# A second-layer head pair in another TensorE order: gate halves between key, value and query products, attention steps at written places

## The chip, the cores and the metric

One core of one Trainium2 chip. The metric is device time in microseconds (us): the median of 3 runs of the kernel before is 784.22 us (781.72 to 784.26). Engines are named as in the profile: PE is TensorE, DVE is VectorE, ACT is ScalarE, POOL is GpSimd, SP is the engine that issues the weight loads.

## The reference, cut to what matters

The model is a two-layer trunk over 512 tokens of width 1024. The first layer is an mLSTM mixer with memory cross-attention. From its output a compressed latent for keys and values is computed, and the second layer is latent attention with 8 heads:

```python
h = rmsnorm(x, norm_g)
q_lat, z, mq, mz = split_cols(h @ w_in, [Q_LORA, B_WIDTH, MEM_WIDTH, MEM_WIDTH])
q = (rmsnorm(q_lat, q_lat_g) @ w_q_up).reshape(bsz, s, B_HEADS, QK_HEAD)
q = rmsnorm(q, q_gain)                      # then rope on the last 64 columns
attn = chunk_causal_attention(q, k_sh, v_sh).reshape(bsz, s, B_WIDTH)
y_b = attn * jax.nn.silu(z)
return x + jnp.concatenate([y_b, y_mem], axis=-1) @ w_out
```

Keys and values (k_sh, v_sh) come from `rmsnorm(c_kv) @ w_kv_b`. A head has 128 plain columns and 64 rope columns in q and k, and 128 in v. The mask is causal in chunks of 64, worked in query blocks of 128. Only the order of this second layer's work is changed, no arithmetic.

## The kernel before, in words

All products run in fp32r with operands split in a high and a low part: `prod` issues high by high, high by low and low by high, three matmuls for each block of the sum. A weight is loaded by SP into `wr` (2 buffers), multiplied by a gain on POOL where there is one (L146), and split by ACT (high part, `wh`, L130) and DVE (low part, `wl`, L131), 2 buffers each.

The second layer works on 4 pairs of heads. What a pair needs is written as Python generators; each `yield` ends a step:

- `b_kv(p)`: keys and values of a pair, 4 steps, one for each 128 tokens (acc tiles of 512 columns). ACT and DVE take them out, norm them, and POOL scales the rope part (L911).
- `b_q(p)`: queries, 4 steps (384 columns). DVE copies the plain part (L949), ACT copies the rope part and sums squares (L951, L190), POOL applies rope (L845 to L848).
- `b_z(p, c)`: the gate product of head c, in two halves of 4 blocks each, then silu (L203, L204).
- `b_T(p, name, h)`: PE transposes of keys or queries (L923) into a `tp` tile, then ACT and DVE split them into `qk` tiles. With h = 2 it is the rope part of both heads (L928); its way out is longer: ACT copy (L931), for keys a DVE copy (L933), and a DVE subtraction (L934), once for each head.
- `b_attn(p)`: attention in 9 steps. Step n computes the scores of unit n (softmax on DVE, ACT, DVE: L977, L322, L324, L332, L333, L335), transposes the probabilities of unit n - 2 into a `tp` tile (L987; taken out by L991 or L993) and, when a head's three units are through, multiplies by the values (L1000).

PSUM tiles are few: `acc` has 4 buffers, `att` 2, `tp` 2. The transposed probabilities of a head lie in one tile of tag `e`, which has one buffer, so head 1's first block can be taken out only when head 0's product with the values is done. These lines hold the spacing of the attention steps:

```python
units = [(h, tiles) for h in range(2) for tiles in ((0, 1), (2,), (3,))]
lag = 2
for n in range(len(units) + lag + 1):
    if n < len(units):
        scores(*units[n])
    if 0 <= n - lag < len(units):
        trans(*units[n - lag])
    m = n - lag - 1
    if m >= 0 and m % 3 == 2:
        values(m // 3)
    yield
```

`weave(main, side, plan)` runs one step of main, then plan[i] steps of side. Tile's scheduler orders each engine's instructions from its own timeline, except inside `tc.manual_schedule(engines={PE})`, where PE keeps the order of the program. In the kernel before, pair 0, pair 1 and the attention of pair 0 are ordered by the scheduler; the products of pairs 2 and 3, the attention of pairs 1 to 3 and the output projection are in the written order.

Of the kernel before, what the change touches and what calls it, by code (L numbers as in the profile page):

```python
# [40 lines left out]
def weave(main, side, plan=()):  # L41
    for i, _ in enumerate(main):
        for _ in range(plan[i] if i < len(plan) else 1):
            next(side, None)
    for _ in side:
        pass


def chain(*gens):
    for g in gens:  # L50
        yield from g
# [8 lines left out]
def trunk(ctx: ExitStack, tc: tile.TileContext, pv_d, pos_d, x_d, memT_d, wmem_d, wg_d, wa_d, woa_d,  # L60
# [131 lines left out]
    def proj_T(w, hT, ps):  # L192
        for k in range(0, KT, 4):
            prod([(ps, sub(hT, slice(None), j), sub(w, slice(None), j), False) for j in range(k, k + 4)],
                 k == 0, k == 4)
            yield
# [568 lines left out]
    mT, _ = load_memT(False)  # L765
# [113 lines left out]
    def b_z(p, c):  # L879
        d = pairs.setdefault(p, {})  # L880
        if c == 0:
            d["z"] = st([P, 2, S], ("z4", "mv")[p % 2])
        sz = d["z"]
        w = load(wb_d[8 + 2 * p + c], KT, P, pv[:, _PV["bn"]:_PV["bn"] + KT])
        ps = acc()
        yield from proj_T(w, hT, ps)
        silu2(sz[:, c], ps)
        yield

    def b_kv(p):  # L890
        d = pairs.setdefault(p, {})
        kns = st([P, NT, 256], "s4", 2)
        krs = s2([P, NT, P])
        d["v"] = vt = st([P, NT, 256], ("gt", "mkT")[p % 2])
        d["ks"] = kns, krs
        w = load(wkvb_d[p], 2, 512)
        for t in range(NT):
            ps = acc()
            prod([(ps, lat(ckT, k, t), sub(w, slice(None), k), True) for k in range(2)], True, True)
            V.tensor_copy(kns[:, t], ps[:, 0:256])  # L900
            A.activation(vt[:, t], ps[:, 256:512], AF.Copy)
            ss = tiny([P, 2])
            for h in range(2):
                sqsum(kns[:, t, h * P:(h + 1) * P], ss[:, h:h + 1])
            V.tensor_scalar(ss, ss, sspe[:, t:t + 1], None, op0=ALU.add)
            r2 = tiny([P, 2])
            rpow(r2, ss, 1.0 / 192, EPS, 2)
            for h in range(2):
                hs = slice(h * P, (h + 1) * P)
                V.tensor_scalar(kns[:, t, hs], kns[:, t, hs], r2[:, h:h + 1], None, op0=ALU.mult)  # L910
                G.tensor_scalar(krs[:, t, h * 64:(h + 1) * 64], kb[:, t], r2[:, h:h + 1], None, op0=ALU.mult)  # L911
            yield

    def b_T(p, name, h):

        d = pairs[p]
        main, rp = d["ks" if name == "k" else "qs"]
        tp = tps()
        if h < 2:
            pair = d.setdefault(name + "n", [])  # L920
            pair.append(st([P, 2, S], "qk", 4, F32R))
            for t in range(NT):
                PE.transpose(tp[:, t * P:(t + 1) * P], main[:, t, h * P:(h + 1) * P], ident)  # L923
            split(pair[h][:, 0], pair[h][:, 1], tp, gg[:, 2:3] if name == "k" else None)
            return
        d[name + "r"] = r = st([P, 2, S], "v", 2, F32R)
        for t in range(NT):
            PE.transpose(tp[:, t * P:(t + 1) * P], rp[:, t], ident)  # L928
        for h in range(2):
            hs, other = slice(h * 64, (h + 1) * 64), slice(64 - h * 64, 128 - h * 64)  # L930
            A.activation(r[hs, h], tp[hs], AF.Copy)  # L931
            if name == "k":
                V.tensor_copy(r[other, h], r[hs, h])  # L933
            V.tensor_tensor(out=(kl[hs, h] if name == "k" else r[other, h]), in0=tp[hs], in1=r[hs, h].bitcast(F32),  # L934
                            op=ALU.subtract)

    def b_q(p):
        d = pairs[p]
        d["rq"] = rqp = st([P, NT, 2], "rqp", 2)
        w = load(wqup_d[p][:, 0:768], 2, 384), load(wqup_d[p][:, 768:1152], 1, 384)  # L940
        qns = st([P, NT, 256], "s4", 2)
        qrs = s2([P, NT, P])
        d["qs"] = qns, qrs
        ssq = tiny([P, NT, 2])
        for t in range(NT):
            ps = acc([P, 384])
            prod([(ps, lat(qlT, k, t), sub(w[k // 2], slice(None), k % 2), True) for k in range(3)], True, True)
            p3 = ps.rearrange("p (a b) -> p a b", a=2)
            V.tensor_copy(qns[:, t].rearrange("p (a b) -> p a b", a=2), p3[:, :, 0:P])  # L949
            qx = st([P, 2, 64], "qx", 2)  # L950
            A.activation(qx, p3[:, :, P:192], AF.Copy)  # L951
            for h in range(2):
                sqsum(p3[:, h], ssq[:, t, h:h + 1])
            rope(qrs[:, t].rearrange("p (a b) -> p a b", a=2), qx, 0, st([P, 2, 64], "qt", 2),
                 lambda i, a, b, t=t: tabs[:, i, t, a:b].unsqueeze(1).broadcast_to([P, 2, b - a]))
            yield
        rpow(rqp.rearrange("p a b -> p (a b)"), ssq.rearrange("p a b -> p (a b)"), 1.0, 192 * EPS, 8)

    def b_attn(p):
        kn, qn, kh, qr, vt, sz, rqp = (pairs[p][n] for n in ("kn", "qn", "kr", "qr", "v", "z", "rq"))  # L960
        prs, pTs = {}, {}

        def scores(h, tiles):
            ps = acc() if p < 3 and tiles[0] == 2 else att()
            views = []
            for j, i in enumerate(tiles):
                n = (i + 1) * P
                m = max(n, 256)
                qs = slice(i * P, (i + 1) * P)
                pt = ps[:, j * 256:j * 256 + m]  # L970
                prod([(pt, (qn[h][:, 0, qs], qn[h][:, 1, qs]), (kn[h][:, 0, :m], kn[h][:, 1, :m]), True)],
                     True, False)
                PE.matmul(pt, qr[:, h, qs], kh[:, h, :m], start=False, stop=False)
                PE.matmul(pt, qr[:, h, qs], kl[:, h, :m], start=False, stop=True)
                views.append(pt[:, :n])
            for v in views:
                V.memset(v[0:64, -64:], -1.0e30)  # L977
            prs[h, tiles] = softmax_rows(views, rqp[:, tiles[0]:tiles[-1] + 1, h])

        def trans(h, tiles):  # L980
            if tiles[0] == 0:
                pTs[h] = st([P, 1280], "e", 1)
            tp = tps()
            n = 0
            for i, pr in zip(tiles, prs[h, tiles]):
                for c in range(i + 1):
                    PE.transpose(tp[:, n:n + P], pr[:, c * P:(c + 1) * P], ident)  # L987
                    n += P
            o = tiles[0] * (tiles[0] + 1) // 2 * P
            if tiles[0] == 2:  # L990
                A.activation(pTs[h][:, o:o + n], tp[:, :n], AF.Copy)  # L991
            else:
                V.tensor_copy(pTs[h][:, o:o + n], tp[:, :n])  # L993

        def values(h):
            ps = att()
            for i in range(NT):
                for c in range(i + 1):
                    o = (i * (i + 1) // 2 + c) * P
                    PE.matmul(ps[:, i * P:(i + 1) * P], vt[:, c, h * P:(h + 1) * P], pTs[h][:, o:o + P],  # L1000
                              start=c == 0, stop=c == i)
            gate_out(yT, 2 * p + h, ps, sz[:, h])
# [11 lines that stand above are left out]
            yield  # L1014

    def b_pair(p):
        yield from b_kv(p)
        yield from b_q(p)
        todo = [(n, h) for h in range(3) for n in "kq"]
        for _ in chain(b_z(p, 0), b_z(p, 1)):  # L1020
            yield
            b_T(p, *todo.pop(0))

    drain(b_pair(0))
    weave(b_pair(1), b_attn(0), (0,) * 5)
    x1b = []

    def residual():
        x1b.extend(load_x(x1_d, nc.sync))
        yield from ()  # L1030
# [4 lines left out]
        A.dma_start(out_d[t * P:(t + 1) * P, half * 512:(half + 1) * 512], o)  # L1035

    with tc.manual_schedule(engines={mybir.EngineType.PE}):
        weave(chain(*(b_pair(p) for p in range(2, 4)), residual(), out_proj(wob_d, yT, b_done)),
              chain(*(b_attn(p) for p in range(1, 4))), ((0,) * 5 + (1,) * 9) * 2)


_OUTS = [((1, S, D), 'float32')]
# [100 lines left out]
```

## Time and profile before

| | |
|---|---|
| median of 3 runs | 784.22 us (781.72 to 784.26) |
| profiled execution | 780.85 us |
| its span in the trace | 779.1 us |
| PE busy | 760.0 us (98%) |
| DVE busy | 497.6 us (64%) |
| ACT busy | 401.7 us (52%) |
| POOL busy | 185.1 us (24%) |

A profile is one execution. Its span runs from the first to the last recorded instruction; 1.75 us of the execution's time lie around it. PE's busy time is modelled from pipelined matmuls, so the reader should look at its idle stretches and at what ended them more than at the 98%.

### The profile page before, as it was taken

What the parts mean: (1) busy time and instruction counts of PE and PEld (TensorE: products, weight loads), DVE (VectorE), ACT (ScalarE), POOL (GpSimd) and SP (SyncE); (2) the same over time, 40 slices, a digit from 0 to 9 for tenths busy, and PEclk for the clock granted to TensorE, in tenths of its full rate; (3) what the DMA queues carried; (4) which work ended last, traced back from release to release, by engine and by line L of the source; (5) the groups of instructions that cost most, each with busy time, mean ns of one, the idle gap of its engine ahead of it and who ended that gap; (6) DMA issues with size and microseconds to landing.
All of it is one profiled execution on the core that took longest, in us unless ns stands there. A gap on an engine that the chain in (4) does not pass through costs nothing.

```text
span 779.1 us, 11004 instructions
## 1 busy us (share of the span) xinstructions
PE 760.0 (98%) x3956; PEld 651.6 (84%) x3956; DVE 497.6 (64%) x978; ACT 401.7 (52%) x940; POOL 185.1 (24%) x286
## 2 busy tenths in 40 slices
PE   7999999999999999999999999999998999999997
PEld 5798887888888888888888888999787888888886
DVE  7753499738768746756434545497678787885432
ACT  4855656436546435546334636467656565644220
POOL 5311010001110101001002175250975461900000
PEclk9999999999999999999999999999999999999999
DMA  9322220322132223225434532222322111511141
GB/s 336 125 89 82 82 82 29 108 82 82 54 109 67 95 84 107 76 87 161 158 141 150 174 109 84 60 62 59 100 65 58 55 52 36 187 55 55 60 157 54
DMA packets 25190, 75.35 MB, mean 97 GB/s; under 512 B 2864, under 2 KB 3504, under 8 KB 25136
## 3 DMA queue, kind: packets, MB, share of 16 engines
q1 hardware_dynamic: 23568, 72.39, 28.1%
q10 hardware_dynamic: 1440, 2.25, 0.8%
q8 instruction: 31, 0.51, 0.3%
q14 instruction: 23, 0.19, 0.1%
q0 software_dynamic: 128, 0.01, 0.0%
HBM read 70.44 MB, written 4.19 MB: 96 GB/s over the span
## 4 chain that ended last, share of the span: by engine, by line
PE 82%; DVE 11%; ACT 2%; issue 1%; POOL 1%; DVEq 0%; ACTq 0%; POOLq 0%
PE acc L160 45%; PE acc L165 23%; PE att L160 3%; PE att L1000 2%; PE att L165 2%; DVE wl L131 2%; PE tp L987 1%; DVE tiny L322 1%; DVE kl L613 1%; PE tp L923 1%; DVE s L335 1%; PE att L699 1%; PE att L700 1%; PE att L698 1%; DVE s L910 1%
## 5 line engine op out<-in xcount | busy, mean ns | idle before, releaser
L131 DVE TENSOR_TENSOR wl<-wr,wh 128x1024 fp32r<-128x1024 f32 (+5 forms) x117 | 140.5, 1202 | 156.8 <-ACT wh L130 132.6
L130 ACT ACTIVATE wh<-wr 128x1024 fp32r<-128x1024 f32 (+5 forms) x117 | 117.8, 1009 | 138.8 <-PE acc L160 114.4
L160 PE MATMUL acc<-wh,hTl 128*128 128x512 f32 (+4 forms) x352 | 123.6, 361 | 0.0
L160 PE MATMUL acc<-wh,hTh 128*128 128x512 f32 (+4 forms) x352 | 123.2, 362 | 0.3 <-ACT hTh L133 0.3
L160 PE MATMUL acc<-hTh,wh 128*128 128x512 f32 x256 | 101.6, 397 | 0.0
L160 PE MATMUL acc<-hTl,wh 128*128 128x512 f32 x256 | 100.5, 393 | 0.0
L165 PE MATMUL acc<-wl,hTh 128*128 128x512 f32 (+4 forms) x352 | 88.6, 359 | 0.0
L160 PE MATMUL acc<-wh,yTh 128*128 128x512 f32 x192 | 75.0, 394 | 0.0
L160 PE MATMUL acc<-wh,yTl 128*128 128x512 f32 x192 | 74.8, 390 | 0.0
L160 PEld LDWEIGHTS acc<-wh,hTh 128*128 128x128 f32 x352 | 65.2, 188 | 9.8 <-ACT hTh L133 0.7
L160 PEld LDWEIGHTS acc<-wh,hTl 128*128 128x128 f32 x352 | 65.5, 188 | 8.2
L165 PE MATMUL acc<-hTh,wl 128*128 128x512 f32 x256 | 69.3, 391 | 0.0
L165 PEld LDWEIGHTS acc<-wl,hTh 128*128 128x128 f32 x352 | 61.7, 188 | 8.9
L146 POOL TENSOR_TENSOR wr<-wr,pv 128x1024 f32<-128x1024 f32 (+2 forms) x24 | 42.6, 1776 | 87.7 <-DMA wr<-in_wb_dram 44.7
L165 PEld LDWEIGHTS acc<-hTh,wl 128*128 128x128 f32 x256 | 47.8, 188 | 9.9
L160 PEld LDWEIGHTS acc<-hTl,wh 128*128 128x128 f32 x256 | 48.2, 188 | 9.1
L160 PEld LDWEIGHTS acc<-hTh,wh 128*128 128x128 f32 x256 | 48.1, 188 | 9.1
L165 PE MATMUL acc<-wl,yTh 128*128 128x512 f32 x192 | 53.3, 389 | 0.0
L185 POOL TENSOR_SCALAR tiny<-tiny 128x2 f32<-128x2 f32 (+4 forms) x36 | 9.9, 276 | 164.3 <-ACT junk L190 52.3
L160 PE MATMUL acc<-wh,u 128*128 128x384 f32 (+1 forms) x160 | 38.9, 367 | 3.4 <-ACT junk L190 2.3
L165 PEld LDWEIGHTS acc<-wl,yTh 128*128 128x128 f32 x192 | 36.0, 188 | 7.4
L160 PEld LDWEIGHTS acc<-wh,yTh 128*128 128x128 f32 x192 | 36.1, 188 | 7.2
(285 smaller groups left out, 1467.9 us busy)
## 6 DMA issues: line engine op xcount, KB each, us to landing
wr<-in_wa_dram SPq DMA_DIRECT2D x46, 512.0 KB, 3.2
wr<-in_wb_dram SPq DMA_DIRECT2D x16, 512.0 KB, 3.5
wr<-in_woa_dram SPq DMA_DIRECT2D x12, 512.0 KB, 3.3
wr<-in_wob_dram SPq DMA_DIRECT2D x12, 512.0 KB, 3.2
wr<-in_wmem_dram SPq DMA_DIRECT2D x8, 512.0 KB, 3.3
yTh<-in_wmem_dram SPq DMA_DIRECT2D x6, 512.0 KB, 6.9
s<-in_memT_dram SPq DMA_DIRECT2D x8, 256.0 KB, 3.9
yTl<-in_x_dram SPq DMA_DIRECT2D x4, 512.0 KB, 9.2
```

The lines of the kernel that those rows point to most:

```text
L130: A.activation(hi, src, AF.Copy)
L131: V.tensor_tensor(out=lo, in0=src, in1=hi.bitcast(F32), op=ALU.subtract)
L146: G.tensor_tensor(out=r3, in0=r3, in1=gain.unsqueeze(2).broadcast_to([P, nk, ncol]), op=ALU.mult)
L160: PE.matmul(ps, x if lhs else w_[0], w_[0] if lhs else x, start=start and id(ps) not in seen, stop=False)
L165: PE.matmul(ps, a_[0] if lhs else w_[1], w_[1] if lhs else a_[0], start=False, stop=stop and left[id(ps)] == 0)
L185: G.tensor_scalar(t, ss, mul, add, op0=ALU.mult, op1=ALU.add)
L322: V.tensor_reduce(mx[:, j:j + 1], ps, axis=AX.X, op=ALU.max)
L335: V.tensor_scalar(out[j], out[j], sm[:, j:j + 1], None, op0=ALU.mult)
L613: V.scalar_tensor_tensor(out=u[:, d:], in0=raw[:, :S - d], scalar=col("cw", (3 - d) * 16 + j), in1=u[:, d:], op0=ALU.mult, op1=ALU.add)
L698: PE.matmul(ps[:, :258], ph[:, blk(c, i)], v[0][:, c], start=c == 0, stop=False)
L699: PE.matmul(ps[:, :258], low(c, i), v[0][:, c], start=False, stop=False)
L1000: PE.matmul(ps[:, i * P:(i + 1) * P], vt[:, c, h * P:(h + 1) * P], pTs[h][:, o:o + P], start=c == 0, stop=c == i)
```

## The change

In the kernel before, a pair's steps are: 4 of keys and values, 4 of queries, then 6 of gates with one `b_T` after each of them (k0, q0, k1, q1, k2, q2). The attention steps of the pair before follow steps 5 to 13, one each.

After, a pair has 14 steps in a written list: gate half, kv, kv, gate half, kv, kv, q, q, q, q, then k0 and k2, gate half with k1 and q0, gate half with q2, and q1. A gate's second half and its silu are now one step. The attention steps are placed by a plan: two behind step 5, one each behind steps 6, 7 and 8, two behind step 9, none behind 10, one each behind 11 and 12, none behind 13. Pair 1 and the attention of pair 0 move into the part in which PE keeps the written order.

```diff
@@ def b_z(p, c):
-        yield from proj_T(w, hT, ps)
+        m = proj_T(w, hT, ps)
+        next(m)
+        yield
+        drain(m)
         silu2(sz[:, c], ps)
         yield
@@ def b_pair(p):
-        yield from b_kv(p)
-        yield from b_q(p)
-        todo = [(n, h) for h in range(3) for n in "kq"]
-        for _ in chain(b_z(p, 0), b_z(p, 1)):
+        kv, q, z = b_kv(p), b_q(p), chain(b_z(p, 0), b_z(p, 1))
+        for g, *ts in ((z,), (kv,), (kv,), (z,), (kv,), (kv,), (q,), (q,), (q,), (q,), (q, ("k", 0), ("k", 2)),
+                       (z, ("k", 1), ("q", 0)), (z, ("q", 2)), (q, ("q", 1))):
+            next(g, None)
+            for t in ts:
+                b_T(p, *t)
             yield
-            b_T(p, *todo.pop(0))
 
     drain(b_pair(0))
-    weave(b_pair(1), b_attn(0), (0,) * 5)
@@ with tc.manual_schedule(engines={mybir.EngineType.PE}):
-        weave(chain(*(b_pair(p) for p in range(2, 4)), residual(), out_proj(wob_d, yT, b_done)),
-              chain(*(b_attn(p) for p in range(1, 4))), ((0,) * 5 + (1,) * 9) * 2)
+        weave(chain(*(b_pair(p) for p in range(1, 4)), residual(), out_proj(wob_d, yT, b_done)),
+              chain(*(b_attn(p) for p in range(4))), (0, 0, 0, 0, 0, 2, 1, 1, 1, 2, 0, 1, 1, 0) * 3)
```

## Rows read from the trace of the kernel before

**Rows 1.** Busy time of each engine, three stretches; then granted clock, DMA.

```profile
541.90:607.50 65.60, 61.76 (x325) 53.71 (x324) 47.13 (x111) 42.43 (x133) 44.60 (x74) 0.97 0.22 67
607.50:655.30 47.80, 45.63 (x287) 40.50 (x286) 39.59 (x91) 28.72 (x82) 20.35 (x36) 1.00 0.17 52
655.30:696.20 40.90, 39.72 (x235) 34.73 (x234) 32.86 (x82) 25.01 (x75) 21.14 (x36) 1.00 0.35 115
```

**Rows 2.** Waits of PE, 540 to 697 us: total us, times, longest.

```profile
PE acc L160 <- ACT junk L190: 2.3, 1, 2.3
PE tp L987 <- DVE s L335: 1.6, 4, 0.6
PE tp L928 <- DVE e L993: 1.3, 1, 1.3
PE tp L837 <- DVE u L134: 0.9, 1, 0.9
```

**Rows 3.** Busy time and granted clock in stretches of 2 us.

```profile
586.00:588.00 2.00, 1.30 (x6) 1.30 (x7) 1.94 (x10) 1.42 (x8) 1.82 (x6) 0.87 0.00 0
588.00:590.00 2.00, 2.00 (x10) 2.00 (x9) 1.52 (x6) 2.00 (x8) 2.00 (x5) 0.50 0.00 0
590.00:592.00 2.00, 2.00 (x12) 1.87 (x12) 2.00 (x6) 2.00 (x7) 1.06 (x3) 0.78 0.00 0
```

**Rows 4.** Timeline of PE in pair 3: start, duration, line, tile, count.

```profile
667.74 0.51 PE L160 MATMUL acc<-qk,qk 128*128 128x384 f32 x2
...
668.62 1.20 PE L160 MATMUL acc<-wh,u 128*128 128x384 f32 x6
...
670.17 0.63 PE L160 MATMUL att<-qk,qk 128*128 128x512 f32 x2
...
682.09 0.70 PE L160 MATMUL att<-qk,qk 128*128 128x512 f32 x2
...
683.32 0.49 PE L987 MATMUL tp<-ident,s 128*128 128x128 f32 x3
683.65 2.40 PE L1000 MATMUL att<-e,gt 128*128 128x128 f32 x20
685.88 0.60 PE L923 MATMUL tp<-ident,s 128*128 128x128 f32 x4
686.24 0.47 PE L160 MATMUL acc<-hTh,wh 128*128 128x512 f32 x1
...
689.09 0.49 PE L987 MATMUL tp<-ident,s 128*128 128x128 f32 x3
```

**Rows 5.** Timelines of PE and DVE: two softmax chains, from scores to probabilities.

```profile
666.07 0.27 PE L974 MATMUL att<-kl,v 128*128 128x256 f32 x1
...
681.12 0.34 PE L974 MATMUL acc<-kl,v 128*128 128x384 f32 x1
...
670.59 1.46 DVE L335 TENSOR_SCALAR s<-s,tiny 128x128 f32<-128x128 f32 x2
...
685.07 0.42 DVE L335 TENSOR_SCALAR s<-s,tiny 128x384 f32<-128x384 f32 x1
```

**Rows 6.** Timeline of DVE behind pair 3's first value product.

```profile
686.08 0.56 DVE L993 COPY e<-tp 128x384 f32<-128x384 f32 x1
...
687.24 0.75 DVE L134 SCALAR_TENSOR_TENSOR qk<-tp,gg,qk 128x512 fp32r<-128x512 f32 x1
```

**Rows 7.** Timelines of PE, ACT, DVE: rope keys from transposes to last subtraction.

```profile
618.62 0.63 PE L928 MATMUL tp<-ident,s 128*128 128x128 f32 x4 [1.27 <-DVE e L993]
...
652.29 0.60 PE L928 MATMUL tp<-ident,s 128*128 128x128 f32 x4
...
655.46 1.22 ACT L931 ACTIVATE v<-tp 64x512 fp32r<-64x512 f32 x2 [1.95 <-DVE kl L934]
...
624.84 0.69 DVE L934 TENSOR_TENSOR kl<-tp,v 64x512 fp32r<-64x512 f32 x1
...
656.53 0.69 DVE L934 TENSOR_TENSOR kl<-tp,v 64x512 fp32r<-64x512 f32 x1
```

## The prediction

> **What bounds the kernel now.** I read the busy time of the engines by stretch first. The change touches only what lies between 541.9 and 696.2 us of the span. The reader is to see there that PE is the engine with the least idle time in every stretch, at 3.84, 2.17 and 1.18 us [rows 1], and that DVE is busy 72, 83 and 80% of them. So PE's instructions are the path, and what an order can win is PE's idle time: 7.2 us together. No instruction of arithmetic is added or removed, so PE's work stays.
>
> Second I read what ended PE's waits [rows 2]. The largest, 2.3 us, is for ACT's sums of squares, which hold an accumulator of the queries; 1.3 us is for a copy of transposed probabilities; four waits of at most 0.6 us are for the normed probabilities. What is left of the first stretch, 3.84 - 2.28 = 1.56 us, is waiting for the transposed query latents, most of it shown as L837.
>
> Third I read the clock in short stretches [rows 3]. Behind the wait of 2.28 us PE ran at 0.50 of its clock, the 1.2 GHz level; before and after it stood at 1.00, or 2.4 GHz. The three rows lose 0.26 + 1.00 + 0.44 = 1.7 us of full speed. The waits of 1.3 us and less lost none: the stretches that hold them stand at 1.00 [rows 1], apart from the first, whose loss is this one.
>
> So 7.2 + 1.7 = 8.9 us is all that can be recovered.
>
> The Trainium skill says the same of the clock (TensorE: Matmul & The Clock Gate, Part 1: The HAM clock gate): the slow level is the default and activity lifts it, so an idle PE falls back. The trace agrees, with 0.50 behind 2.28 us of idling.
>
> **The change part by part.** What it removes:
>
> Gates first in pair 0. Pair 0 stays with the scheduler, but half a gate now comes ahead of its first key and value products. Gate products need only the normed input and a weight, so 5.7 us of PE work (two halves of 2.85, 686.24 to 689.09 [rows 4]) can lie under the wait for the query latents. The wait is 1.56 us; I take all of it as gone. If the gate weight comes late, it stays: 0 to 1.56.
>
> Pair 1 in written order. The 2.28 us wait falls among the four query products that the scheduler put close together with scores. In the written list, attention steps lie between the query products, as in pairs 2 and 3 before. I take the wait, its 1.7 us of clock and the 1.27 us of L928 as gone. Pairs 2 and 3 lose their small waits, 2.17 - 1.27 = 0.9 and 1.18 us. They are replaced by what follows; each new wait is counted for pairs 1, 2 and 3.
>
> What it adds, three waits in a pair:
>
> (a) First transposes of probabilities. Two attention steps now stand together, so behind the first scores PE has only unit 1 (667.74 to 668.62, 0.88), one query product (668.62 to 670.17, 1.55) and unit 2 (682.09 to 683.32, 1.23) before it wants the probabilities of unit 0: 3.66 us [rows 4]. The softmax chain took 4.0 us (681.12 + 0.34 to 685.07 + 0.42) and 5.7 us (666.07 + 0.27 to 670.59 + 1.46) [rows 5]. The wait is 0.4 or 2.0 us. I take 0.4: with key products and a gate between, DVE comes to this place less loaded than in the longer row, where it had all four key tiles just behind it. Bounds 0 and 2.0. The queue behind it on PE is everything, since PE keeps the written order.
>
> (b) k0 behind head 0's values. Before, a whole gate half lay between most uses of the two tp tiles. Now two attention steps stand together behind the last query product: transposes of head 1, values, transposes. The copy of the first of these must wait for the values, because tag e has one buffer. It began 0.20 us behind the value product (685.88) and took 0.56 [rows 4, 6], 0.76 in all; PE has 0.33 us of transposes (683.32 to 683.65) to put there. k0 needs this tile, so it waits 0.43; I take 0.4. If DVE stands one 1 us instruction behind, 1.4.
>
> (c) k0, k2, then k1, q0 and transposes: five fillings of two tp tiles with one gate half between. k2's tile is long in use: ACT waited 1.95 us for DVE between its two halves, and from the first transpose to the last subtraction it took 4.93 us in pair 2 (652.29 to 657.22) and 6.91 in pair 1 (618.62 to 625.53) [rows 7]. From k2's start PE has k2 0.36, the gate half 2.85 and k1 0.36, 3.57 us [rows 4], before q0 wants that tile. The wait is 1.36 to 3.34. Before, this tile's next user came behind four key and some query products, so nobody waited. If q0 did not wait, the transposes behind it would: k1's tile takes from its start to 687.24 + 0.75, 2.11 us for the same kind (685.88), less 0.72 for k1 and q0, again 1.4 [rows 4, 6]. So the place costs 1.4 either way; I take 1.4. Lower bound 1.1, if DVE and ACT stand ready; upper 3.3.
>
> Weights move with the order. SP issues the same loads. With two buffers, a gate's second weight can be split when the queries' first is through, and there are 1.23 + 0.33 + 2.23 + 0.33 us and more for it; the next pair's key weight has values, b_T and a gate half, 5.4 us or more. I allow 0.3 us in a pair for a split that comes late, bounds 0 and 1. POOL's gain product of the gates stays at two in a pair. The residual's loads sit behind the same last key and query products; the output projection follows these some 15 us later, so they stay hidden.
>
> Sum: a pair waits 0.4 + 0.4 + 1.4 + 0.3 = 2.5 us, three pairs 7.5. Recovered 8.9. Net -1.4 us: span 779.1 to 777.7, execution 780.85 to 779.45. The profiled execution lies 3.4 us under the median of 784.22, so the same step on the median gives 782.8 us.
>
> **The rivals.** First, clearly faster. DVE and ACT catch up whenever PE stands, so a wait at one place shortens the next: (a) 0, (b) 0.4, (c) 1.1. Then 1.5 in a pair, 4.5 in all, -4.4 us: 779.8 us; with none of the three it would be -8.9, 775.3. For it speaks that DVE is 80 to 83% busy [rows 1], so the backlog is local; against it, that two tp tiles are a matter of count, not of load.
>
> Second, slower, by one mechanism: k2's tile. If its way out takes pair 1's 6.91 us, q0 waits 3.3 us, longer than the 2.28 us behind which the clock fell, and each such wait costs 1.7 us of clock besides. A pair then loses 0.4 + 0.4 + 3.3 + 0.3 + 1.7 = 6.1 us, three 18.3, net +9.4: 793.6 us. It is slower by more than 0.5% from (8.9 + 3.9) / 3 = 4.3 us in a pair. For it: behind the value product DVE also has the gated output, k0 and the last softmax to do. Against it: 4.93 us in the pair that already had the written order.
>
> The Trainium skill has a rule that speaks for this rival (Perfetto Trace Analysis, Optimization Strategy): the same gap repeating on the engine that should be saturated can mean too few buffers for the next tile. The trace of before shows no wait on a tp tile that repeats; by the rule (c) would come in every pair, in the same place.
>
> Third, the change doesn't do what it says in pair 1. The 2.28 us wait came of ACT being late, and ACT and DVE get the same work in another place. If the wait and its clock loss return, 4.0 of the 8.9 us are not recovered: net +2.6, 786.8 us.
>
> **How the numbers follow.** About 0.5%, 3.9 us, is what a measurement of this kernel can tell from no change. The forecast, 782.8 with its own range of 780.5 to 786, has 0.38. Clearly faster has 0.32, the slower rival, in one pair or in all, 0.20, the wait that returns 0.10. Faster by over 0.5% (under 780.3) is the first rival and a rim of the forecast, 0.35; slower (over 788.1) the second and a little of the third, 0.22; the rest, 0.43, is within. The range is cut where a tenth is left on each side: 776.5 in the faster case, 790 in the slower.
>
> **What would show it.** PE idle between 541.9 and the start of the output projection should fall from 7.2 to about 7 us or less, with no 0.50 clock in it. The wait for L837 and the one for L190 should be gone. In each of pairs 1 to 3 there should be a wait before L987 of about 0.4 us, one before L923 for L993 of about 0.4, and one before L923 for L934 or L134 of about 1.4. The prediction is wrong if the scheduler's order of DVE brings k2's subtractions early, so that (c) is under 0.7, or late enough that the clock falls; or if pair 0 grows waits that I have at nothing.

## The result, and the profile after

The changed kernel takes 806.47 us (median of 4 runs, 806.11 to 807.38), the kernel before 783.82 us on the same chip (4 runs, 781.72 to 784.26): a ratio of 1.0295, 95% interval 1.0279 to 1.0312. It is 22.7 us slower, where 1.4 us faster was forecast. Lines of the changed file stand 3 below those of before (L987 is now L990, L923 L926, L993 L996).

| profiled execution | before | after |
|---|---|---|
| span | 779.1 us | 804.3 us |
| PE busy | 760.0 us | 765.8 us |
| span less PE busy | 19.1 us | 38.5 us |

PE runs the same 3956 matmul instructions in both. So of 25.2 us more span, 19.4 us are idle time of PE, and in the other 5.8 us PE is busy longer with the same work, which goes with the lower clock. Three stretches of the changed kernel hold together the 847 matmuls of the three of [rows 1], though the first reaches further into the work; they show both (length, busy time of PE, PEld, DVE, ACT, POOL, then granted clock, DMA):

```profile
542.20:628.10 85.90, 73.89 (x391) 63.93 (x390) 59.12 (x126) 47.69 (x142) 42.17 (x74) 0.92 0.18 54
628.10:676.80 48.70, 40.92 (x234) 36.11 (x233) 33.33 (x81) 25.46 (x75) 20.30 (x36) 0.93 0.15 45
676.80:721.50 44.70, 38.35 (x222) 33.96 (x220) 29.11 (x78) 23.84 (x73) 18.57 (x35) 0.96 0.29 97
```

PE is idle 12.0, 7.8 and 6.4 us. DVE's busy share fell to 69, 68 and 65%, but only because the stretches are longer: it is busy 121.6 us in them, where it was 119.6 before. The waits of PE between 540 and 722 us name the place; they answer to [rows 2]:

```profile
PE tp L990 <- DVE s L335: 20.5, 6, 8.4
PE tp L926 <- DVE kl L937: 3.2, 3, 1.1
PE acc L160 <- ACT junk L190: 1.2, 1, 1.2
PE tp L926 <- DVE s L913: 0.6, 1, 0.6
PE tp L931 <- ACT e L994: 0.5, 3, 0.2
```

They sum to 26.0 us, where before PE was idle 7.2 us in the same work; the difference of 18.8 us is nearly all of the 19.4. PE's timeline has the single waits in brackets, here one of pair 0, the three of unit 0, and a few others:

```profile
563.80 0.51 PE L160 MATMUL acc<-hTh,wh 128*128 128x512 f32 x1 [1.21 <-ACT junk L190]
...
597.68 0.88 PE L990 MATMUL tp<-ident,s 128*128 128x128 f32 x3 [8.43 <-DVE s L335]
...
618.25 0.63 PE L926 MATMUL tp<-ident,s 128*128 128x128 f32 x4 [1.05 <-DVE kl L937]
...
640.78 0.40 PE L977 MATMUL att<-kl,v 128*128 128x512 f32 x1
647.21 0.95 PE L990 MATMUL tp<-ident,s 128*128 128x128 f32 x3 [6.04 <-DVE s L335]
647.81 2.27 PE L160 MATMUL acc<-wh,u 128*128 128x384 f32 x6
...
694.50 0.95 PE L990 MATMUL tp<-ident,s 128*128 128x128 f32 x3 [4.61 <-DVE s L335]
```

In each of pairs 1 to 3 PE stands 8.43, 6.04 and 4.61 us before the first transposes of probabilities, 19.08 us in all, and then runs on slowly: six matmuls that took 1.20 us [rows 4] take 2.27. The windows around pair 2's wait show the clock at 0.50, its 1.2 GHz level, when PE starts again:

```profile
638.00:642.00 4.00, 3.18 (x17) 2.61 (x15) 1.39 (x5) 0.75 (x4) 3.56 (x4) 1.00 0.47 131
642.00:646.00 4.00, 0.00 (x0) 0.00 (x0) 3.06 (x9) 1.09 (x4) 3.74 (x8) 0.69 0.01 4
646.00:650.00 4.00, 2.79 (x10) 2.71 (x11) 3.21 (x12) 2.33 (x8) 1.65 (x4) 0.50 0.00 2
650.00:654.00 4.00, 4.00 (x28) 4.00 (x27) 1.53 (x7) 2.26 (x9) 1.48 (x4) 0.96 0.00 0
```

What does DVE do meanwhile? Its timeline in pair 2, from the mask of unit 0's scores to the normed probabilities that PE waits for:

```profile
637.89 0.11 DVE L980 MEMSET att<- 64x64 f32 x1
638.54 0.11 DVE L980 MEMSET acc<- 64x64 f32 x1 [0.53 <-PE acc L977]
640.05 0.42 DVE L952 COPY s<-acc 128x256 f32<-128x256 f32 x1 [1.40 <-PE acc L165]
640.40 0.22 DVE L908 TENSOR_SCALAR tiny<-tiny,sspe 128x2 f32<-128x2 f32 x1
641.29 2.20 DVE L913 TENSOR_SCALAR s<-s,tiny 128x128 f32<-128x128 f32 x2 [0.68 <-POOL tiny L186]
643.50 0.11 DVE L980 MEMSET att<- 64x64 f32 x1
643.53 0.54 DVE L322 TENSOR_REDUCE tiny<-att 128x1 f32<-128x128 f32 x2
644.11 0.16 DVE L324 SCALAR_TENSOR_TENSOR tiny<-tiny,rqp 128x2 f32<-128x2 f32 x1
...
645.64 0.54 DVE L913 TENSOR_SCALAR s<-s,tiny 128x128 f32<-128x128 f32 x2 [0.90 <-POOL tiny L186]
...
646.84 0.58 DVE L335 TENSOR_SCALAR s<-s,tiny 128x128 f32<-128x128 f32 x2
```

The scores are masked at 638.00, but the softmax's first instruction, L322, runs at 643.53. Ahead of it in DVE's row stand the masks of units 1 and 2 (L980), the copy of a query tile that PE has yet to finish (L952), the add for the last key tile (L908), and the norm of the key tile before (L913), which waits for POOL's root (L186). From L322 to the end of L335 it then takes 643.53 to 647.42, 3.89 us, near the chain of 4.0 us of [rows 5]. So 643.53 - 638.00 = 5.53 of the 6.04 us are standing in line; the rest is the little by which the chain exceeds its cover. Of the 5.53 us DVE is idle 0.53 and 1.40 us for PE's scores of unit 1 and for the query tile, and 0.68 us for the root; 1.66 us are what L913 takes too long, and the rest is work. The last key tile's norm (645.64) then stands inside the chain. POOL's timeline says why the root is late:

```profile
638.27 1.90 POOL L146 TENSOR_TENSOR wr<-wr,pv 128x1024 f32<-128x1024 f32 x1 [1.88 <-DMA wr<-in_wb_dram]
640.25 0.19 POOL L185 TENSOR_SCALAR tiny<-tiny 128x2 f32<-128x2 f32 x1
640.53 0.73 POOL L186 TENSOR_TENSOR tiny<-tiny,mhalf 128x2 f32<-128x2 f32 x1
641.23 1.90 POOL L146 TENSOR_TENSOR wr<-wr,pv 128x1024 f32<-128x1024 f32 x1
```

The root's input was there at 637.89, but POOL stood until 638.27 at a gate's gain product (L146) whose weight had not landed, and worked 1.90 us on it, before it took the root, 2.36 us late. The second gain product then ran beside L913, which took 2.20 us where the same two products took 0.54 us at 645.64. The Trainium skill has this (SBUF — State Buffer, SBUF: two separate sides): DVE and GpSimd share one pair of ports, and where both need it, the instruction that has it keeps it to its end. The trace agrees: L913 ends 0.36 us behind the L146 that ran beside it. In pairs 1 and 3 L913 stands ahead of L322 too, with 0.32 and 0.92 us for the root; in pair 1 another 1.50 us for a root lie inside the chain.

### The profile page after: what moved, and what is told of

It is laid out like the page before. It is cut to its first block, busy times and chain, and to the rows that moved or that the text cites. A ratio compares the mean times of both kernels' runs of the same rounds, so it can differ in the third digit from the quotient of the medians.

```text
span 804.3 us, 11003 instructions
## 1 busy us (share of the span) xinstructions
PE 765.8 (95%) x3956; PEld 656.2 (82%) x3956; DVE 498.1 (62%) x978; ACT 401.6 (50%) x940; POOL 182.8 (23%) x286
## 4 chain that ended last, share of the span: by engine, by line
PE 80%; DVE 9%; POOL 3%; ACT 2%; issue 2%; DMA 1%; POOLq 0%
PE acc L160 45%; PE acc L165 22%; PE att L160 3%; DVE wl L131 2%; PE att L165 2%; PE att L1003 1%; DVE tiny L322 1%; DMA wr<-in_wb_dram 1%; PE tp L990 1%; POOL wr L146 1%; DVE s L335 1%; DVE kl L613 1%; POOL tiny L186 1%; PE att L699 1%; PE att L700 1%
## 5 line engine op out<-in xcount | busy, mean ns | idle before, releaser
L146 POOL TENSOR_TENSOR wr<-wr,pv 128x1024 f32<-128x1024 f32 (+2 forms) x24 | 42.4, 1768 | 66.9 <-DMA wr<-in_wb_dram 28.0
L160 PEld LDWEIGHTS acc<-wh,yTl 128*128 128x128 f32 x192 | 36.1, 188 | 7.0
```

Source lines behind the costliest of these rows:

```text
L146: G.tensor_tensor(out=r3, in0=r3, in1=gain.unsqueeze(2).broadcast_to([P, nk, ncol]), op=ALU.mult)
L160: PE.matmul(ps, x if lhs else w_[0], w_[0] if lhs else x, start=start and id(ps) not in seen, stop=False)
```

## The experiments

Two theories were tried first. By the theory of the queue, the softmax of unit 0 is late for what stands ahead of it on DVE, the norm of the last key tiles. By the theory of the spacing, it is late because the new plan puts units 0 and 1 together and leaves too little of PE's work before the first transposes.

**The old even plan with the new list.**

```diff
-              chain(*(b_attn(p) for p in range(4))), (0, 0, 0, 0, 0, 2, 1, 1, 1, 2, 0, 1, 1, 0) * 3)
+              chain(*(b_attn(p) for p in range(4))), ((0,) * 5 + (1,) * 9) * 3)
```

> The changed kernel with the attention steps spread as in the kernel before (one behind each of steps 5 to 13), the pair's new list and the longer written part kept. Theory S (spacing): the wait before the first transposes of probabilities, 8.4, 6.0 and 4.6 us, comes of two attention steps standing together; with 5.2 us of PE work in place of 3.7 it goes, as in the kernel before (at most 0.6 us), and the kernel falls to about 786 us. Theory Q (queue): DVE holds the softmax behind the norm of the last key tiles, which waits for POOL; a query product more in between takes only its own 1.6 us from each wait, which stay at 3 to 6.8 us, and the kernel at about 800 us.

Measured: 831.62 us, ratio 1.0623 (1.0587 to 1.0658). The last unit's scores now come behind k2, and as all pairs share the one tile `kl`, they wait for and read the next pair's low parts of the rope keys. Of PE's waits:

```profile
PE tp L990 <- DVE s L335: 15.3, 3, 5.9
PE att L977 <- DVE kl L937: 11.9, 3, 4.0
PE tp L931 <- DVE e L996: 5.5, 3, 1.8
PE tp L926 <- DVE e L996: 3.6, 2, 1.8
```

The waits at unit 0 stay, 5.92, 5.78 and 3.62 us, though units 0 and 1 are now apart. They lie in the 3 to 6.8 us of the theory of the queue: the spacing alone is not it. The total missed both expectations. Some 23 us of new waits, the three lower lines and 2.3 us more, are those of a late plan: its last steps put scores and transposes among the b_T tiles.

**No gain product on POOL.** L146 is left out for the gates, so their weights are not scaled.

```diff
-        w = load(wb_d[8 + 2 * p + c], KT, P, pv[:, _PV["bn"]:_PV["bn"] + KT])
+        w = load(wb_d[8 + 2 * p + c], KT, P)
```

> The changed kernel without the gain product of the gate weights on POOL in the head pairs (this leaves the norm's gain out of the gates). Theory G (a part of Q: POOL is late because two gain products of 1.9 us, the first waiting for its load, stand ahead of the reciprocal roots of the key tiles): the three waits fall to at most 2 us each and the kernel to about 788 us. Theory S: the waits stay, the kernel stays within 3 us of 806.

Measured: 793.60 us, ratio 1.0133 (1.0102 to 1.0165). The waits at unit 0 fall from 8.43, 6.04, 4.61 to 5.14, 3.03, 3.04 us. So POOL's products are 7.9 of the 19.1 us, less than I expected; 11.2 us stay without them.

**Key tiles first, same plan.** All four key and value tiles come first and both gate halves behind them, so that 5.7 us of gates lie between the last key tile and unit 0; units, plan and cover are the same.

```diff
-        for g, *ts in ((z,), (kv,), (kv,), (z,), (kv,), (kv,), (q,), (q,), (q,), (q,), (q, ("k", 0), ("k", 2)),
+        for g, *ts in ((kv,), (kv,), (kv,), (kv,), (z,), (z,), (q,), (q,), (q,), (q,), (q, ("k", 0), ("k", 2)),
```

> The changed kernel with the four key and value products first and the two gate halves behind them, so that 5.7 us of gate products lie between the last key tile and the first scores; the PE work between first scores and first transposes stays at 3.7 us. Theory Q: the key norms are through before the softmax comes to DVE, the waits fall to the 0.4 to 2 us that the softmax chains of the kernel before give, the kernel to about 787 us. Theory S: the waits stay at 4.6 us and more, the kernel at about 806 us.

Measured: 792.28 us, ratio 1.0109 (1.0066 to 1.0152). The waits at unit 0 fall to 2.54, 1.65 and 1.53 us. Of PE's waits (this line has those at unit 4 too; it was 20.5 us):

```profile
PE tp L990 <- DVE s L335: 7.4, 6, 2.5
```

That is the queue's mark: the cover is the same 3.66 us and no work is left out, only the key norm and the gain products are further off. The time fell less than to the expected 787 us. In pair 2 the last key norm still stands ahead of the softmax, with 1.46 us for its root; the clock still falls, to 0.58 between 590 and 594 us; and the wait for k2's tile, L926 behind L937, grew from 1.06 to 2.0 us in two pairs.

**The boundary alone.** The kernel before, with nothing but pair 1 and pair 0's attention put into the written order.

```diff
-    weave(b_pair(1), b_attn(0), (0,) * 5)
...
-        weave(chain(*(b_pair(p) for p in range(2, 4)), residual(), out_proj(wob_d, yT, b_done)),
-              chain(*(b_attn(p) for p in range(1, 4))), ((0,) * 5 + (1,) * 9) * 2)
+        weave(chain(*(b_pair(p) for p in range(1, 4)), residual(), out_proj(wob_d, yT, b_done)),
+              chain(*(b_attn(p) for p in range(4))), ((0,) * 5 + (1,) * 9) * 3)
```

> The kernel before with only one part of the change: pair 1 and the attention of pair 0 in the written order, with the old list of a pair and the old plan. If the scheduler's order of pair 1 was the loss (waits of 2.3 and 1.3 us and 1.7 us of clock), the kernel gains some 4 us, 780 us. If the written order by itself costs, it is slower than 784, by 2 us or more.

Measured: 786.47 us, ratio 1.0027 (1.0010 to 1.0043). PE's timeline keeps the wait that the written order should have removed, larger, and has it in pair 2 as well:

```profile
589.90 2.29 PE L160 MATMUL acc<-wh,u 128*128 128x384 f32 x6 [3.58 <-ACT junk L190]
...
633.18 1.72 PE L160 MATMUL acc<-wh,u 128*128 128x384 f32 x6 [2.22 <-ACT junk L190]
```

So the third rival holds for this part of the change, which alone costs 2.1 us: in pairs 1 and 2 ACT's squares are late. Pair 3 has the same list and no such wait, and nor had pairs 2 and 3 of the kernel before, so the written order by itself doesn't make it; why it comes in these two is not shown.

**Softmax at a higher priority.**

```diff
-            prs[h, tiles] = softmax_rows(views, rqp[:, tiles[0]:tiles[-1] + 1, h])
+            with tc.high_priority():
+                prs[h, tiles] = softmax_rows(views, rqp[:, tiles[0]:tiles[-1] + 1, h])
```

> The changed kernel with the instructions of the softmax given a higher priority than their neighbours, so that VectorE takes the softmax of unit 0 before the norm of the last key tiles; TensorE's order is the changed one. If the waits L990 behind L335 (8.43, 6.04, 4.61 us) come from the order on VectorE alone (the softmax stands behind the key norm, which stands behind GpSimd's root and the gain products), they fall to at most 2 us each, about 13 us in all with their clock come back, and the time is 788 to 794 us. If the softmax is late for its own data or its own length (cover of 3.66 us too short), the waits stay near 6 us each and the time near 806 us. If the key norm, put later, holds up k0 instead, L926 behind L937 or L913 grows from 1.06 us each to over 2, and the time stays at 798 us or more.

Measured: 806.77 us, ratio 1.0303 (1.0281 to 1.0324), with waits of 8.75, 6.26 and 4.65 us at unit 0. This one decides nothing, because DVE's order at the place did not change. In its timeline of pair 2, L913 still stands before L322:

```profile
641.79 2.20 DVE L913 TENSOR_SCALAR s<-s,tiny 128x128 f32<-128x128 f32 x2 [0.90 <-POOL tiny L186]
...
644.03 0.54 DVE L322 TENSOR_REDUCE tiny<-att 128x1 f32<-128x128 f32 x2
```

**Norm of the keys on POOL.**

```diff
-                V.tensor_scalar(kns[:, t, hs], kns[:, t, hs], r2[:, h:h + 1], None, op0=ALU.mult)
+                G.tensor_scalar(kns[:, t, hs], kns[:, t, hs], r2[:, h:h + 1], None, op0=ALU.mult)
```

> The changed kernel with the norm of the keys (line 913) on GpSimd, behind its own root, and no longer on VectorE; TensorE's order is the changed one, and nothing of the gain products or of the cover of 3.66 us is touched. If the softmax of unit 0 is late because it stands on VectorE behind a key norm that waits for GpSimd's root, the waits L990 behind L335 (8.43, 6.04, 4.61 us) fall to at most 2 us each, the clock of the stretches behind them comes back, and the time is 787 to 793 us, unless k0 now waits for GpSimd by more than the 1.06 us a pair that it waits in the changed kernel. If unit 0 is late for the length of its own chain or for the cover alone, the waits stay at 4.5 us and more, and the time at 803 us or more.

Measured: 807.54 us, ratio 1.0304 (1.0282 to 1.0327). The waits at unit 0 fell to 3.88, 5.38 and 3.78 us, 13.0 in all, but not to 2. DVE's timeline of pair 2 shows that the rest of the key chain is still ahead of the softmax, the add L908, which waits for ACT's squares and is then itself held, 1.61 us where it took 0.22:

```profile
643.52 1.61 DVE L908 TENSOR_SCALAR tiny<-tiny,sspe 128x2 f32<-128x2 f32 x1 [0.23 <-ACT junk L190]
645.05 0.61 DVE L322 TENSOR_REDUCE tiny<-att 128x1 f32<-128x128 f32 x2
```

POOL ran the second gain product from 643.22 to 645.12 there. Before that, DVE stands 0.53, 1.40 and 0.78 us for PE's scores of units 1 and 2 and its query tile, all ahead of the softmax. And pair 0 paid with POOL: a new wait of 3.02 us for L914, and 2.92 us for L190 where it was 1.21. My expectation was wrong in taking the product alone for the whole row. The time is that of its rival, but as the row stayed it doesn't speak for the chain's own length.

**No norm chain at all.** A constant stands for the root.

```diff
-            V.tensor_scalar(ss, ss, sspe[:, t:t + 1], None, op0=ALU.add)
-            r2 = tiny([P, 2])
-            rpow(r2, ss, 1.0 / 192, EPS, 2)
+            r2 = mhalf[:, 0:2]
             for h in range(2):
-                hs = slice(h * P, (h + 1) * P)
-                V.tensor_scalar(kns[:, t, hs], kns[:, t, hs], r2[:, h:h + 1], None, op0=ALU.mult)
```

> The changed kernel without the norm of the keys: the add of line 908, the root of lines 185 and 186 and the product of line 913 are left out (a constant stands for the root in line 914; the squares on ScalarE stay). TensorE's order, the gain products and the cover of 3.66 us are those of the changed kernel. If the softmax of unit 0 is late because VectorE's queue holds it behind the last key tiles' norm, the waits L990 behind L335 fall from 8.43, 6.04 and 4.61 us to what the cover and the softmax's own chain leave, the 0.4 us of the prediction and at most 1 us with the gain products beside it; with the clock that comes back and 1.06 us a pair left at the next tile, the time is 783 to 789 us. If something else holds it (GpSimd's products at the shared port, or the chain's own length), waits of 2 us or more stay, and the time is 793 us or more.

Measured: 784.35 us, ratio to the kernel before 1.0016 (1.0002 to 1.0029). With TensorE's order and the gain products as in the changed kernel, the 22 us are gone: the key norm's chain, in DVE's row ahead of the softmax, makes them. The key tiles first, where no work is left out, say the same. Span and PE busy are 783.6 and 760.6 us, so idle time fell by 15.5 us and the work by 5.2. The waits at unit 0 are 1.98, 2.13 and 1.00 us (in pairs 1 and 2 in two parts), over the 1 us that I expected at most. Of PE's waits (lines stand 4 higher here, and unit 4 is in it):

```profile
PE tp L986 <- DVE s L335: 6.9, 8, 2.0
```

DVE's timeline of pair 2 shows why they are not less:

```profile
625.76 0.62 DVE L322 TENSOR_REDUCE tiny<-att 128x1 f32<-128x128 f32 x2
...
626.49 1.53 DVE L324 SCALAR_TENSOR_TENSOR tiny<-tiny,rqp 128x2 f32<-128x2 f32 x1
...
629.45 1.89 DVE L335 TENSOR_SCALAR s<-s,tiny 128x128 f32<-128x128 f32 x2
```

L322 now follows the masks at once, and the chain takes 625.76 to 631.34, 5.6 us, of which L324 (0.16 in the changed kernel) and L335 (0.58) have 2.7 us too much, both beside a product L146; without that it would fit the cover. In size this is the upper bound of (a), 5.7 us and a wait of 2.0 us. One thing went with the chain: DVE's row now has the copy of the query tile (L948) and the masks of units 1 and 2 behind L322, not ahead of it, so that the 0.53 and 1.40 us for which DVE stood there are gone too. The run shows what the chain costs with the row that comes of it, not its instructions alone.

**Unit 0 earlier.** The list with key tiles first, and unit 0 behind the first gate half.

```diff
-              chain(*(b_attn(p) for p in range(4))), (0, 0, 0, 0, 0, 2, 1, 1, 1, 2, 0, 1, 1, 0) * 3)
+              chain(*(b_attn(p) for p in range(4))), (0, 0, 0, 0, 1, 1, 1, 1, 1, 2, 0, 1, 1, 0) * 3)
```

> The four key and value tiles first, then both halves of the gate product, and unit 0 of attention one step earlier, behind the first half: the softmax of unit 0 is covered by 2.85 + 0.88 + 1.55 + 1.23 = 6.5 us of TensorE's work by the durations of the changed kernel, where it was 3.66. If a long enough cover and an undisturbed VectorE are what the place of unit 0 lacks, the waits L990 behind L335 (2.54, 1.65, 1.53 us with the same list and the cover of 3.66) fall to under 0.5 each; against the 792.3 us of that list this is some 5 us, so 785 to 789 us. If scores ahead of the key norm's last root are themselves held up (a wait of the scores on the eviction or on a bank), a new wait of 1 to 3 us stands before them and the time stays at 791 to 794 us.

Measured: 786.84 us, ratio 1.0049 (1.0033 to 1.0065), as expected. Unit 0's first transposes wait no more, in any pair. PE's timeline of pair 2 has them at 632.19 without a bracket; what is left are 5.1 us on the two tp tiles and 2.6 us at a late unit 4, shown here, and some 5 us in smaller places (the first scores in pair 1, splits of weights):

```profile
632.19 0.49 PE L990 MATMUL tp<-ident,s 128*128 128x128 f32 x3
...
644.67 0.52 PE L990 MATMUL tp<-ident,s 128*128 128x128 f32 x3 [0.73 <-DVE s L335]
...
651.67 0.63 PE L926 MATMUL tp<-ident,s 128*128 128x128 f32 x4 [2.00 <-DVE kl L937]
```

**Three lists against what is left.** The first moves q2 and q1 into the next pair, so that fewer transposed tiles follow each other (in short, against the list with the early unit):

```diff
-        for g, *ts in ((kv,), (kv,), (kv,), (kv,), (z,), (z,), (q,), (q,), (q,), (q,), (q, ("k", 0), ("k", 2)),
-                       (z, ("k", 1), ("q", 0)), (z, ("q", 2)), (q, ("q", 1))):
+        late = [("q", 2), ("q", 1)] if p else []
+        for g, *ts in ((kv,), (kv,), (kv,), (kv,), (z,), (z,), (q,), (q,), (q,), (q,), (z,), (q, ("k", 0)),
+                       (no, ("k", 2), ("k", 1)), (z, ("q", 0))):
             next(g, None)
+            if late:
+                b_T(p - 1, *late.pop(0))
...
+              chain(*(b_attn(p) for p in range(4))), (0, 0, 0, 0, 1, 1, 1, 1, 1, 2, 1, 1, 0, 0) * 3)
```

> As the kernel with the early unit, and no two transposed tiles follow each other without other work of a microsecond or more between: k0 behind a query tile, k2 and k1 behind a gate product, q0 behind the next, q2 and q1 behind the first two key and value tiles of the next pair. By the theory that the back-to-back fill of the two transposed tiles costs the waits L926 behind L937 (1.06 to 2.0 us each) and the second transposes' 0.46 us, these go too: some 1.5 to 2.5 us a pair less, 780 to 785 us. By the rival that what was saved there comes back as waits of the last query tile's norm or of attention's later units on q1 and q2, waits of 1 us or more stand at the scores of units 3 and later and the time is 786 us or more.

Measured: 787.71 us, ratio 1.0068 (1.0047 to 1.0090). The three waits for L937 are gone; 4.25 us at the rope tile of pair 0's queries, and 1.66 and 2.62 us at unit 0, came instead. The second, spread wider (in short, for pairs 1 to 3; pair 0 has a list of its own):

```diff
...
+            plan = ((kv,), (kv,), (kv,), (kv,), (z,), (z,), (q,), (q,), (q,), (q,), (z,), (q, ("k", 0)),
+                    (no, ("k", 2)), (z, ("k", 1)), (no, ("q", 0)))
...
+              chain(*(b_attn(p) for p in range(4))), (0, 0, 0, 0, 1, 1, 0, 1, 1, 1, 1, 1, 1, 1, 0) * 3)
```

> As the kernel with its transposed tiles apart, but one step more between the scores of units 1 and 2 and no two units in one step, k0, k2, k1 and q0 each with an attention step or a gate half between, and pair 0, which has no attention to lie between, with its key tiles between the query products. If the waits of 4.25 us (pair 0's k2 tile), 1.66 and 2.62 us (unit 0's transposition) and 1.01 us (the last pair's scores) are what is left, 9.5 us and the clock behind them go, and the time is 775 to 781 us, below the kernel before. If VectorE's queue only puts the same lateness in front of another unit, waits of 1 us or more stand at later transpositions or scores, and the time is 784 us or more.

Measured: 785.39 us (12 runs), ratio 1.0019 (1.0004 to 1.0035), within the bound of 0.5%. Unit 0 waits nowhere. The wait at pair 0's late tile stayed, 3.77 us (it is q2's, not k2's as the expectation has it), and 1.58 and 1.61 us before unit 4 are new. The same kernel with the norm on POOL:

> The spread kernel with the norm of the keys on GpSimd as well. If VectorE's wait for GpSimd's root still costs there, 1 to 3 us less than the spread kernel; if it no longer does, the same within 2 us; if GpSimd, which does the gain products and the rope keys too, gets late with the norms, k0's transposition waits 1 us or more a pair and it is 3 us or more slower.

Measured: 788.90 us, ratio 1.0075 (1.0055 to 1.0095), 3.5 us over the spread kernel. That is the time that I expected if GpSimd gets late, but no wait at k0 shows it; the new wait, of 2.19 us, is at a softmax, and its cause stays open. The third takes pair 0 as in the changed kernel and moves unit 4 behind a gate half (in short, against the spread kernel):

```diff
...
-                    (no, ("k", 2)), (z, ("k", 1)), (no, ("q", 0)))
+        steps = ((kv,), (kv,), (kv,), (kv,), (z,), (z,), (q,), (q,), (q,), (q,), (z,), (q, ("k", 0)), (z,), (no,),
+                 (no, ("k", 2)), (no, ("k", 1), ("q", 0)))
```

> The spread kernel with pair 0 as in the changed kernel (so nothing of its tiles lies in pair 1), unit 4's transposition behind the last gate half and no longer behind k0 and unit 3's, and k2 behind unit 5's. If the waits of the spread kernel (3.77 us at pair 0's late tile, 1.58 and 1.61 us behind the eviction of line 996, 0.67 us three times) are its cost, some 8 us go and the time is 776 to 781 us, below the kernel before. If they are what VectorE's late queue puts at the next place, waits of 1 us or more stand elsewhere in each pair and the time is 783 us or more.

Measured: 787.57 us, ratio 1.0054 (1.0038 to 1.0070). Each of its pairs has 1.60 us at L926 behind L937 again, and 2.31 us for L190 is back in pair 0. By my own rule the lateness only moved. No list here beats the kernel before; the best comes within 0.2% of it.

## Why the prediction was wrong

**What bounds.** PE's instructions are the path, as said, and its idle time and its slower work are the whole of the difference (19.4 + 5.8 of 25.2 us).

**The step that failed is (a).** It took 0.4 us, at most 2.0, for "DVE comes to this place less loaded". Measured: 8.43, 6.04 and 4.61 us. Its cover was right: 3.66 us is that of the trace (in pair 2 unit 0's scores end at 637.57, unit 2's at 641.18, 3.61 us). The chain takes 3.89 us, or 5.6 when the port is held. That the 4.0 us met this was luck, for they were the chain of unit 4; the 5.7 us of [rows 5] were unit 0's own. Wrong was to start the chain at the end of the scores. DVE's load was not the point, and it did the same work as before; it took instructions in their row, and those ahead of the softmax waited for others: for PE's next scores and query tile and for POOL's root, and this one behind a gain product. In the old list two query products lay between the last key tile and unit 0; the new plan put unit 0 directly behind it. Without that chain the same order takes 784.35 us. This is 1.6 us over my forecast, but with less work on DVE and POOL, and against the kernel before of its own runs (782.87 us) it is 1.5 us slower where I had 1.4 faster: that the rest of the forecast was right is not shown.

The queue was in the trace of before. Unit 0's scores in pair 3 are masked at 666.72, and DVE's and POOL's timelines go on:

```profile
667.14 0.68 DVE L910 TENSOR_SCALAR s<-s,tiny 128x128 f32<-128x128 f32 x2 [0.42 <-POOL tiny L186]
667.75 0.61 DVE L322 TENSOR_REDUCE tiny<-att 128x1 f32<-128x128 f32 x2
...
669.81 1.90 POOL L146 TENSOR_TENSOR wr<-wr,pv 128x1024 f32<-128x1024 f32 x1
```

The softmax stood 1.03 us behind a key norm that waited for its root, and its L335 took 1.46 us [rows 5] beside a gain product, where it takes 0.58 alone. Without the two, 5.7 us would be about 3.8.

**The clock.** I priced a fall of the clock only in the second rival. Three waits of over 4 us and those in pair 0 lie ahead of the 5.8 us of slower work, 5.2 of which came back without the norm chain.

**(b)** was 0.4 us at k0, for DVE's copy; k0 waits nowhere, and 0.16 us at k2 behind it, for ACT's copy (L994), were measured. 0.46 to 0.47 us that I had not priced stand at head 1's second transposes in each pair, behind their softmax. **(c)** was 1.4 us with a lower bound of 1.1; measured 1.05, 1.06 and 1.06, on k2's tile, in every pair and the same place. A kernel in which these tiles lie apart (787.71 us) has no such wait, but waits elsewhere. The Trainium skill's rule that a repeating gap can mean too few buffers (Perfetto Trace Analysis, Optimization Strategy) fits these 1.06 us; the trace does not bear it out for the far larger gap that repeats, at unit 0, most of which went with a chain left out and no buffer added. No run adds a buffer. The allowance of 0.3 us for weights was not needed: PE waits for no split there.

**What it removes.** The L837 wait is gone, but 0.62 us for the key norm and 1.21 us for ACT's squares stand in pair 0 instead, and the clock fell to 0.50 behind them. Pair 1's L190 wait is gone with the new list; with the written order alone it is there, at 3.58 us.

**The rivals.** The slower side had 0.22, for k2's tile, which was not it; no rival had the softmax in line behind another chain. The busy times of [rows 1] can't show a queue, and the question what is queued was asked of PE alone, though DVE's timeline of before had the answer.

What stays open: whether DVE would gain by taking the softmax first. The priority did not change the order there.

## What to carry to other kernels

When work is moved on one engine, list for each other engine what then stands ahead of the moved work's first instruction, and what each of those waits for: an engine that takes instructions in order can be 30% idle and still 5 us late. A long chain over several engines, such as a norm with its root, wants independent work behind it before the next chain starts on the same engine: here 5.7 us of gates took the waits at unit 0 from 19.1 to 5.7 us. A cover worked out from PE's durations is to be held against the time to the end of the chain, from the moment at which the chain's first instruction can get its turn.

## What was not expected of the hardware

POOL's product of 128x1024 held DVE instructions of very different size: a norm of two 128x128 products, 2.20 us for 0.54; an add on 128x2, 1.61 for 0.22; L324 on 128x2, 1.53 for 0.16.

The clock's fall did not follow the length of the wait alone. Behind 1.21 us in pair 0 of the changed kernel, begun 0.33 us after another of 0.62 had ended, the 2 us windows have 0.75, 0.50 and 0.90:

```profile
564.00:566.00 2.00, 2.00 (x8) 1.57 (x8) 1.44 (x2) 0.28 (x3) 2.00 (x4) 0.75 0.54 117
566.00:568.00 2.00, 2.00 (x6) 1.62 (x5) 0.12 (x1) 1.87 (x10) 2.00 (x5) 0.50 0.83 252
568.00:570.00 2.00, 2.00 (x9) 1.62 (x8) 0.78 (x2) 0.33 (x2) 2.00 (x6) 0.90 0.24 94
```

Behind 2.00 us in pair 2 of the kernel with the early unit, it stayed at 1.00:

```profile
650.00:652.00 2.00, 0.33 (x3) 0.36 (x4) 1.56 (x3) 1.05 (x2) 0.00 (x0) 1.00 0.00 0
652.00:654.00 2.00, 1.94 (x12) 1.50 (x11) 1.34 (x3) 0.60 (x1) 0.00 (x0) 1.00 0.00 0
```
